# Attention kernel: VectorE's score cells from jobs further on, chains of eight, earlier casts and transposes

## The chip, the cores and the metric

The kernel runs on one core of a Trainium2 chip. The metric is device time in microseconds (us), from one execution of the whole program; lower is better. Eleven runs of the kernel before gave a median of 397.95 us (397.08 to 401.34).

A core has several engines that each run their own list of instructions in order and meet only through semaphores: TensorE (PE in the profile; PEld is its weight load), VectorE (DVE), ScalarE (ACT), GpSimd (POOL) and the DMA queues, of which SyncE's (SP) and POOL's are used here. An instruction that waits holds up all that stand behind it in its engine's list.

## The reference: grouped-query attention

```python
batch, n_q_heads, n_kv_heads, seq, head_dim = (8, 8, 2, 1024, 64)
for g in range(n_kv_heads):          # four q heads share one k and v head
    scores = scale * np.matmul(q_group, k_group.transpose(0, 1, 3, 2))
    scores_max = np.max(scores, axis=-1, keepdims=True)
    attn = np.exp(scores - scores_max)
    attn = attn / (np.sum(attn, axis=-1, keepdims=True) + 1e-08)
    output[:, q_start:q_end, :, :] = np.matmul(attn, v_group)
```

All is float32, the inputs are normal numbers times 0.1. The kernel leaves the maximum out, since the scores are small, and works in bf16 behind the loads.

## The kernel before, in words

**Jobs and cells.** A q head has 1024 rows; the even and the odd rows ("side") make two jobs of 512 rows, so 8 x 8 x 2 = 128 jobs. A job has eight cells, one for each 128 keys: 1024 cells. A cell's scores are one matmul (`score`, L351): 128 keys on the partitions, 512 q rows on the free axis, in one PSUM bank. The exponentials of a cell then serve as weights of four small matmuls against V with a column of ones (`output_mms`, L414, 128x65), which add up a job's output and its row sums in an `ops` bank. `normalise` (L427, L429) divides, and SP stores the job's 128 KB.

**Two engines make exponentials.** ScalarE takes pairs of cells (kind A; `exps`, L362, 128x1024 from the two-bank tile `aps`, of which there are two). VectorE takes single cells (kind D; `dps`, two banks): `exp_bits` (L371) turns a score into the bits of a power of two in a group tile `pd`, and when a group of GROUP = 4 cells is full, `exp_curve` corrects the mantissa of the whole group in four instructions, a chain: AND into `z` (L386), a line into `y` (L392), a product (L402) and a sum into `pd` (L406). Only then may the cells of the group go to PE.

**The planner.** `make_plan` decides on the host, ahead of the build, which cell goes to which engine and in which order each engine does its work. It keeps a time for PE, ACT and DVE, moves them on by fixed costs (`QK`, `PV`, `EXP`, `P1`, `NORM`, `CHAIN`), and picks the earliest step each time. Its times order the instructions; on the chip nothing waits for a time. In the kernel before, the cells are dealt out in order of their number: the next cell goes to ACT's tile or to DVE's bank, whichever is free first. LIVE_A, LIVE_D and PENDING bound the tiles in flight, and the last 14 cells (ONLY_A) go to ACT. Its 1024 cells become 412 pairs on ACT and 200 cells in 50 chains of four on DVE.

**Loads.** The first k, q and v heads come straight as float32, are cast on chip and turned by PE through the `dps` banks (`first_loads`). All other heads go the long way: a casting DMA from POOL's queue into a bf16 scratch in DRAM (`cast`, L248), from there two transposing DMAs on SP's queue for each head (`transpose`, L260), and for k a further four copies on POOL's queue into the zero-padded set `kset` (`place_k`, L268), for v two copies on SP's queue (`place_v`, L282). Two sets of k and v serve even and odd batches. Each load is put into the order some us of plan time ahead of the head's first cell. A cast that is put in after the first score also waits, through a dependency added by hand, for the last score issued ahead of it in the order ("pace"). In `first_loads` POOL also clears the second k set with two memsets (L309), ahead of all casts but the first.

Of the kernel before, what the change touches and what calls it, by code (L numbers as in the profile page):

```python
# [14 lines left out]
GROUP = 4  # L15


def make_plan(nj, nkc):
# [6 lines left out]
    QK, PV, EXP, P1, NORM = 0.214, 0.143, 0.925, 0.605, 0.57  # L25
    CHAIN = (0.73, 0.73, 1.26, 1.26)
    FROM_PE, FROM_ACT, FROM_DVE = 0.28, 0.18, 0.12
    LIVE_A, LIVE_D, PENDING, ONLY_A = 26, 6, 8, 14
    INF = 1e9
    n = nj * nkc  # L30
# [3 lines left out]
    nxt = 0  # L34
# [7 lines left out]

    def first_free(slots):
        return min(range(len(slots)), key=lambda s: slots[s])

    while normed < nj:
        best = None
        if nxt < n:
            ta = td = INF
            if open_a is not None:  # L50
                ta = max(pe, open_a["t"])
            elif live["A"] < LIVE_A:
                ta = max(pe, min(a_free))
            if pending < PENDING and nxt < n - ONLY_A and (cur or live["D"] < LIVE_D):
                td = max(pe, min(bank))
            t, to_d = (ta, 0) if ta <= td else (td, 1)
            if t < INF:
                best = min(best or (INF,), (t, 1 + to_d, "qk", to_d))
        for i, s in enumerate(open_jobs):
            for c in rem[s]:  # L60
                at = max(pe, ready.get(s * nkc + c, INF))
                if at < INF:
                    best = min(best or (INF,), (at, 3 + i, "pv", (s, c)))
        if len(open_jobs) < 2 and next_job < nj:
            at = max(pe, min(obank_free), min(ready.get(next_job * nkc + c, INF) for c in range(nkc)))
            if at < INF:
                best = min(best or (INF,), (at, 3 + len(open_jobs), "open", next_job))
        for q, p, kind in ((normq, 0, "norm"), (p1q, 1, "p1"), (chainq, 2, "chain")):
            if q:
                best = min(best or (INF,), (max(dve, q[0][0]), p, kind, 0))  # L70
        if cur and nxt >= n - ONLY_A and not p1q:
            best = min(best or (INF,), (dve, 9, "flush", 0))
        t, _, kind, arg = best
        if kind == "qk":
            cell = nxt
            nxt += 1
            pe = t + QK
            if not arg:
# [10 lines left out]
                if len(o["cells"]) == 2 or nxt >= n:  # L89
                    act = max(act, pe + FROM_PE)  # L90
                    ops.append((act, "exp", a_id, tuple(o["cells"])))
                    act += EXP * len(o["cells"]) / 2
# [5 lines left out]
            else:  # L98
                k = first_free(bank)
# [48 lines left out]
        else:  # L148
            _, g, cells, step = chainq.pop(0)
            ops.append((t, "chain", g, len(cells), step))  # L150
            dve = t + CHAIN[step] * len(cells) / GROUP
            if step + 1 < len(CHAIN):
                chainq.insert(0, (dve, g, cells, step + 1))
# [9 lines left out]
def kernel(  # L163
# [27 lines left out]
    PIECE = 256  # L191
    scale = 1.0 / math.sqrt(D)
# [15 lines left out]
    qT_pool = ctx.enter_context(tc.tile_pool(name="qTpool", bufs=8))  # L208
    kT_pool = ctx.enter_context(tc.tile_pool(name="kTpool", bufs=4))
    pa_pool = ctx.enter_context(tc.tile_pool(name="papool", bufs=26))  # L210
    pd_pool = ctx.enter_context(tc.tile_pool(name="pdpool", bufs=6))
# [76 lines left out]

    def first_loads():
# [216 lines left out]
```

The softmax here doesn't subtract the row's maximum and nothing guards it: scores larger than these inputs give would overflow.

## Time and profile before

| | |
|---|---|
| median of 11 runs | 397.95 us |
| the profiled execution's own time | 397.5 us |
| its span, first to last instruction | 395.6 us |
| busy: PE, DVE, ACT, POOL | 365.4, 375.9, 381.3, 87.4 us |
| exponentials on ACT | 412 instructions, 378.8 us |
| first exponential starts, last one ends | 8.18 us, 388.27 us |

The page gives for each engine its busy time, for each group of instructions the count, busy time and mean duration, and the idle time in front of them with what ended it. A group's mean can overlap with the next instruction's start, so a busy sum is smaller than count times mean. The timeline gives start and length of merged pieces in order of time. "SPq" and "POOL ... DMA_DIRECT2D" are the times in which a queue issues a transfer; its landing is later.

### The profile page before, as it was taken

Reading aid. Unit: us, or ns where it says so; the run is one execution under the profiler, and the core shown is the slowest. Engines: PE = TensorE matmul, PEld = TensorE weight load, DVE = VectorE, ACT = ScalarE, POOL = GpSimd, SP = SyncE. Lnnn points to the kernel's source line nnn. Section 1 sums busy time; section 2 is a strip of 40 time slices with the busy share of each in tenths; the row PEclk is TensorE's granted clock in tenths of the full one; section 3 lists DMA queues with packets and bytes.
Section 4 is the critical chain, followed back from the end, with each engine's and each line's share of the span. In section 5 each row is a group of like instructions: output and inputs, shape, how many; then the busy total and the mean of one; then the engine's idle time right before and its main releaser. Section 6 shows DMA issues by size and latency. Waiting matters only on the chain.

```text
span 395.6 us, 12683 instructions
## 1 busy us (share of the span) xinstructions
PE 365.4 (92%) x5043; PEld 232.9 (59%) x5132; DVE 375.9 (95%) x664; ACT 381.3 (96%) x415; POOL 87.4 (22%) x165
## 2 busy tenths in 40 slices
PE   4899999999999999999999999999999999999986
PEld 2455565565656556665656565565655666565655
DVE  4999999999999999999999999999999999999995
ACT  4999999999999999999999999999999999999992
POOL 5340404131041313113141040313113131210000
PEclk9999999999999999999999999999999999999999
DMA  4666967848577795758767677775955977573314
GB/s 106 108 122 110 152 100 136 140 94 150 103 136 133 114 152 99 129 108 151 118 114 127 105 124 146 137 124 109 149 95 117 155 131 138 95 127 82 68 28 94
DMA packets 134890, 46.72 MB, mean 118 GB/s; under 512 B 130848, under 2 KB 132384, under 8 KB 133344
## 3 DMA queue, kind: packets, MB, share of 16 engines
q1 hardware_dynamic: 129408, 29.52, 37.9%
q0 software_dynamic: 4896, 16.13, 28.3%
q8 instruction: 40, 0.66, 0.8%
q10 hardware_dynamic: 528, 0.26, 0.2%
q14 instruction: 18, 0.15, 0.1%
HBM read 27.13 MB, written 28.97 MB: 142 GB/s over the span
## 4 chain that ended last, share of the span: by engine, by line
ACT 67%; DVE 11%; PE 10%; issue 6%; DMA 3%; POOL 1%; SPq 0%
ACT pa L362 67%; PE ops L414 5%; PE aps L351 5%; DVE pd L371 3%; DVE y L402 2%; DVE pd L406 2%; DVE ost L429 1%; PE dps L351 1%; DVE y L392 1%; DMA vf<-in_v_dram 1%; DMA qT<-scr_q 1%; POOL kset L309 1%; DVE z L386 1%; DVE rec L427 1%; DMA scr_q<-in_q_dram 1%
## 5 line engine op out<-in xcount | busy, mean ns | idle before, releaser
L362 ACT ACTIVATE pa<-aps 128x1024 bf16<-128x1024 f32 x412 | 378.8, 1063 | 2.4 <-PE aps L351 1.7
L351 PE MATMUL aps<-qT,kset 128*128 128x512 bf16 x735 | 225.9, 379 | 16.0 <-ACT pa L362 13.6
L414 PEld LDWEIGHTS <-pa 128*128 128x128 bf16 x3296 | 134.6, 97 | 57.4 <-DVE ost L429 0.8
L414 PE MATMUL ops<-vset,pa 128*128 128x65 bf16 x3296 | 143.9, 194 | 3.4
L371 DVE TENSOR_SCALAR pd<-dps 128x512 uint16<-128x512 f32 x200 | 129.7, 681 | 1.9 <-PE dps L351 1.9
L351 PEld LDWEIGHTS <-kset 128*128 128x128 bf16 x1024 | 85.2, 97 | 66.7 <-issue 30.7
L248 POOL DMA_DIRECT2D scr_q<-in_q_dram x63 | 34.5, 547 | 173.7 <-PE aps L351 151.2
L351 PE MATMUL dps<-qT,kset 128*128 128x512 bf16 x200 | 64.3, 379 | 0.9
L406 DVE TENSOR_TENSOR pd<-pd,y 128x2048 uint16<-128x2048 uint16 x50 | 61.2, 1225 | 1.7
L402 DVE TENSOR_TENSOR y<-z,y 128x2048 f16<-128x2048 uint16 x50 | 61.2, 1225 | 1.7
L429 DVE TENSOR_TENSOR ost<-ops,rec 128x256 f32<-128x256 f32 x128 | 54.3, 424 | 4.4
L414 PEld LDWEIGHTS <-pd 128*128 128x128 bf16 x800 | 38.5, 97 | 29.8 <-DVE pd L406 8.1
L268 POOL DMA_DIRECT2D kset<-kT x60 | 32.4, 549 | 75.3 <-DMA kT<-scr_k 72.4
L414 PE MATMUL ops<-vset,pd 128*128 128x65 bf16 x800 | 45.3, 194 | 1.2
L392 DVE TENSOR_SCALAR y<-z 128x2048 f16<-128x2048 uint16 x50 | 34.3, 686 | 0.6
L386 DVE TENSOR_SCALAR z<-pd 128x2048 uint16<-128x2048 uint16 x50 | 34.2, 685 | 0.0
L427 DVE RECIPROCAL rec<-ops 128x4 f32<-128x4 f32 x128 | 22.4, 175 | 2.8 <-PE ops L414 2.3
L248 POOL DMA_DIRECT2D scr_v<-in_v_dram x15 | 7.7, 510 | 8.2 <-PE aps L351 7.4
L248 POOL DMA_DIRECT2D scr_k<-in_k_dram x15 | 8.3, 551 | 5.2 <-PE aps L351 4.0
L321 PE MATMUL dps<-ident,hk 128*128 128x128 bf16 x8 | 1.0, 311 | 5.0 <-DVE hk L313 5.0
L321 PEld LDWEIGHTS <-hk 128*128 128x128 bf16 x8 | 0.8, 140 | 5.0 <-DVE hk L313 5.0
L309 POOL MEMSET kset<- 64x2048 bf16 x2 | 3.6, 1798 | 0.1
(20 smaller groups left out, 9.7 us busy)
## 6 DMA issues: line engine op xcount, KB each, us to landing
out_dram<-ost SPq DMA_DIRECT2D x128, 128.0 KB, 3.0
scr_q<-in_q_dram POOLq DMA_DIRECT2D x63, 128.0 KB, 3.4
kset<-kT POOLq DMA_DIRECT2D x60, 64.0 KB, 2.6
qT<-scr_q SPq DMA_TRANSPOSE x126, 3.7
scr_k<-in_k_dram POOLq DMA_DIRECT2D x15, 128.0 KB, 4.2
scr_v<-in_v_dram POOLq DMA_DIRECT2D x15, 128.0 KB, 4.3
vset<-scr_v SPq DMA_DIRECT2D x30, 64.0 KB, 3.9
kT<-scr_k SPq DMA_TRANSPOSE x30, 3.3
```

The lines of the kernel that those rows point to most:

```text
L248: dma = nc.gpsimd.dma_start(out=scr.rearrange("(p f) -> p f", f=1024), in_=src.rearrange("(p s) d -> p (s d)", s=1024 // D),)
L268: nc.gpsimd.dma_start(out=ksets[b % 2][side * D : (side + 1) * D, g, side, parity * HALF : (parity + 1) * HALF], in_=kT[(b, g)][parity * D ...
L351: last_score[0] = nc.tensor.matmul(dst, lhsT=ksets[b % 2][:, h // HPG, side, c * 128 : (c + 1) * 128], rhs=qT[(b, h)], start=True, stop=Tr ...
L362: nc.scalar.activation(out=pt[:, 0:m], in_=psum.pop(("A", n))[:, 0:m], func=AF.Exp, scale=scale)
L371: nc.vector.tensor_scalar(out=groups[g][:, slot], in0=psum.pop(cell), scalar1=bits_scale, scalar2=bits_bias, op0=ALU.mult, op1=ALU.add,)
L386: nc.vector.tensor_scalar(out=z, in0=pd, scalar1=0x7F, scalar2=None, op0=ALU.bitwise_and)
L392: nc.vector.tensor_scalar(out=y, in0=temps[g][0], scalar1=CURVE_A / 128.0, scalar2=CURVE_B, op0=ALU.mult, op1=ALU.add,)
L402: nc.vector.tensor_tensor(out=y, in0=z, in1=y, op=ALU.mult)
L406: nc.vector.tensor_tensor(out=pd, in0=pd, in1=y, op=ALU.add)
L414: nc.tensor.matmul(ops_of[s][:, qs, :], lhsT=p_of[cell][:, qs * 128 : (qs + 1) * 128], rhs=vsets[b % 2][:, h // HPG, c, :], start=opens an ...
L427: nc.vector.reciprocal(out=rec, in_=o[:, :, D])
L429: nc.vector.tensor_tensor(out=ost, in0=o[:, :, 0:D], in1=rec.unsqueeze(2).to_broadcast([128, NQS, D]), op=ALU.mult,)
```

## The change

- `GROUP` is 8: a chain works on eight cells (4096 elements on each partition). `pd` tiles are 5 of twice the size in place of 6, `z` and `y` grow with them; `pa` has 28 buffers in place of 26, `qT` 10 in place of 8.
- The planner holds each job's cells to be done. ACT takes the next cell of the first job that has any left; VectorE takes the first cells left of a job that lies up to LEAD = 6 jobs further on (growing by one for each three jobs at the start), two of a job at most. A model of the first loads (`loaded`) keeps cells from being planned before 3.5 us, plus 3.0 us for each further q head. The planner's costs are new. Its order now has 411 pairs on ACT, and 202 cells on DVE in 25 chains of eight and a last chain of two.
- A head's first use is that of either job and either engine. Casts of q come 34 to 40 us of plan time ahead of it (28 before), transposes 17 to 21 (17), casts of k and v 46 and 42 ahead of the first use in their group (38 and 33), k's transposes 31 (first batch 19; 27 before), `place_k` 15 (first batch 8; 20 before).
- In `first_loads` k and q come in halves, PE first does 28 matmuls of the identity, which nobody reads (WARM), and the order of casts and copies is another. The memsets of the second k set leave `first_loads` and stand at 20 and 23 us of plan time.

```diff
-GROUP = 4
+GROUP = 8
@@ make_plan
+    LIVE_A, LIVE_D, PENDING, PER_JOB, LEAD, RAMP, AHEAD, FIRST_PV = 28, 5, 16, 2, 6, 3, 0.08, 2.0
+    FIRST_LOAD, EACH_LOAD = 3.5, 3.0
+    def loaded(j):
+        return FIRST_LOAD + EACH_LOAD * (j // 2 - 1) if j > 1 else 0.0
...
+        while job_a < nj and not todo[job_a]:
+            job_a += 1
+        lead = min(LEAD, job_a // RAMP)
+        job_d = max(job_d, job_a + lead)
+        while job_d < nj and (taken[job_d] >= PER_JOB or not todo[job_d]):
+            job_d += 1
...
+            cell = j * nkc + todo[j].pop(0)
@@ first_loads
-        for side in range(2):
-            nc.gpsimd.memset(ksets[1][(1 - side) * D : (2 - side) * D, :, side, :], 0.0)
+        warm = obanks[1].tile([128, 128], FP32, name="ops1")
+        for n in range(WARM):
+            nc.tensor.matmul(warm, lhsT=ident, rhs=ident, start=True, stop=True)
...
+        for half in halves:
+            nc.vector.tensor_copy(out=hk[:, half, 0:2, :], in_=fk[:, half])
+            turn_k(0, half)
+            nc.scalar.copy(
+                out=hq[:, half], in_=fq[:, half].rearrange("p c two d -> p c (two d)")
+            )
+            for c in range(NHC)[half]:
+                nc.tensor.transpose(tq[:, c * 128 : (c + 1) * 128], hq[:, c, :], ident)
@@ the order of the loads
+    for side in range(2):
+        at(20.0 + 3.0 * side, blank_k, side)
...
-            th = first_use[(b * H + h) * 2]
+            th = first_use[b * H + h]
             if (b, h) != (0, 1):
-                at(th - 28.0, cast, ("q", b, h), q[b, h])
+                at(th - (34.0 if b else 40.0), cast, ("q", b, h), q[b, h])
             for n in range(HALF // PIECE):
-                at(th - 17.0 + n, transpose_q, b, h, n)
+                at(th - (21.0 if b else 17.0) + n, transpose_q, b, h, n)
             if h % HPG == 0:
                 g = h // HPG
-                at(th - 38.0, cast, ("k", b, g), k[b, g])
-                at(th - 33.0, cast, ("v", b, g), v[b, g])
+                th = min(first_use[b * H + h + i] for i in range(HPG))
+                at(th - 46.0, cast, ("k", b, g), k[b, g])
+                at(th - 42.0, cast, ("v", b, g), v[b, g])
                 for n in range(HALF // PIECE):
-                    at(th - 27.0 + n, transpose_k, b, g, n)
+                    at(th - (31.0 if b else 19.0) + n, transpose_k, b, g, n)
                 for side in range(2):
                     for parity in range(2):
-                        at(th - 20.0, place_k, b, g, side, parity)
+                        at(th - (15.0 if b else 8.0), place_k, b, g, side, parity)
```

## The prediction

> **What bounds the kernel now.** I read the busy sums first, then the groups, then the timeline at both ends.
>
> ```profile
> PE 365.4 (92%) x5043; PEld 232.9 (59%) x5132; DVE 375.9 (95%) x664; ACT 381.3 (96%) x415; POOL 87.4 (22%) x165
> ...
> L362 ACT ACTIVATE pa<-aps 128x1024 bf16<-128x1024 f32 x412 | 378.8, 1063 | 2.4 <-PE aps L351 1.7
> L371 DVE TENSOR_SCALAR pd<-dps 128x512 uint16<-128x512 f32 x200 | 129.7, 681 | 1.9 <-PE dps L351 1.9
> L406 DVE TENSOR_TENSOR pd<-pd,y 128x2048 uint16<-128x2048 uint16 x50 | 61.2, 1225 | 1.7
> L402 DVE TENSOR_TENSOR y<-z,y 128x2048 f16<-128x2048 uint16 x50 | 61.2, 1225 | 1.7
> L392 DVE TENSOR_SCALAR y<-z 128x2048 f16<-128x2048 uint16 x50 | 34.3, 686 | 0.6
> L386 DVE TENSOR_SCALAR z<-pd 128x2048 uint16<-128x2048 uint16 x50 | 34.2, 685 | 0.0
> ```
>
> ACT and DVE look equally full, but ACT is the bound: its exponentials wait 2.4 us in all, 1.10 of it ahead of the first. One costs 378.8/412 = 0.919 us. The timeline gives the ends and the one real hole:
>
> ```profile
> 4.51 0.43 DVE L313 CAST hk<-f 128x512 bf16<-128x512 f32 x1 [1.42 <-DMA f<-in_k_dram]
> 4.86 0.29 DVE L314 CAST hk<-f 128x256 bf16<-128x256 f32 x1
> 5.82 0.63 PE L327 MATMUL dps<-ident,hq 128*128 128x128 bf16 x4
> 6.49 0.58 ACT L331 COPY qT<-dps 128x512 bf16<-128x512 bf16 x1 [0.94 <-PE dps L327]
> 6.57 3.65 POOL L309 MEMSET kset<- 64x2048 bf16 x2
> 7.13 1.67 PE L351 MATMUL aps<-qT,kset 128*128 128x512 bf16 x4 [0.67 <-ACT qT L331]
> 8.18 10.26 ACT L362 ACTIVATE pa<-aps 128x1024 bf16<-128x1024 f32 x11 [1.10 <-PE aps L351]
> 9.25 0.59 PE L351 MATMUL aps<-qT,kset 128*128 128x512 bf16 x2
> 13.05 2.39 SPq L260 DMA_TRANSPOSE qT<-scr_q  x2
> 18.43 0.59 PE L351 MATMUL aps<-qT,kset 128*128 128x512 bf16 x2 [0.74 <-DMA qT<-scr_q]
> 19.05 3.77 ACT L362 ACTIVATE pa<-aps 128x1024 bf16<-128x1024 f32 x4 [0.61 <-PE aps L351]
> ...
> 385.35 2.92 ACT L362 ACTIVATE pa<-aps 128x1024 bf16<-128x1024 f32 x3
> 389.24 2.63 PE L414 MATMUL ops<-vset,pa 128*128 128x65 bf16 x80
> 392.12 0.42 DVE L429 TENSOR_TENSOR ost<-ops,rec 128x256 f32<-128x256 f32 x1
> ```
>
> So the span is 8.18 (start) + 380.09 (ACT from 8.18 to 385.35 + 2.92 = 388.27) + 7.33 (tail) = 395.6. Of the middle, 378.8 is work, 0.61 the hole at 18.4, where PE waits for the third q head, and 0.7 small change. The run's own time is 397.5, 1.9 above its span; the median of the runs, 397.95, is 0.45 above that.
>
> **The middle: chains of eight.** The chain's cost for eight cells isn't in the trace. The two casts above (512 elements 0.427, 256 elements 0.286) give 0.145 us fixed for an instruction. So a 4096-element AND or line is 2 x 0.685 - 0.145 = 1.225, a product or sum 2 x 1.225 - 0.145 = 2.305. Bounds: no fixed part (1.37 and 2.45, no gain), or two fixed parts (1.08 and 2.16). Instructions fall from 200 to 104: 96 x 0.145 = 13.9 us less; two more cells cost 2 x (0.60 + 0.27 + 0.54) = 2.8 more (0.60 is the pitch of `exp_bits`: two take 1.28 where one takes 0.68). DVE's 375.9 becomes about 365 (between 361 and 379). None of it is on the path by itself: ACT's share only falls from 412 to 411 pairs, 0.92 us. DVE's gain turns into idle time, and its slack against ACT's 378 grows from about 2 to about 13 us. Only at the high end of the bounds would DVE tie with ACT.
>
> The rule on VectorE's fixed latency of an instruction ("VectorE: DVE Perf Modes", section on the TRN2 errata) has a measured fixed term of about 150 cycles, 0.156 us by an estimate at its 0.96 GHz, a little more than my 0.145; the DVE sum would be 1 us lower, and the time the same.
>
> PE keeps its 1024 scores and 4096 output matmuls. At 0.21 a score (two take 0.59 where one takes 0.38) and 0.031 an output matmul (80 in 2.63, of which 0.19 is one's length) that is 215 + 127 = 342 of ACT's 378. D cells now lie up to seven jobs ahead of ACT's, so their outputs are ready when PE comes to them; the 8.1 us that output weights wait for `pd` should go, hidden already.
>
> **The start.** q's second half of cast, transposes and copy sets the first score. The loads are the same bytes; a half of the q cast is about 0.35 (0.62 less 0.27), so it ends near 5.3 where the whole ended at 5.56. But 28 matmuls of the identity now stand ahead on PE: they can begin when the identity is done (2.34) and take about 0.10 each (eight transposes in 0.77 of weight loads), to 5.1 or 5.4. Eight transposes behind them end at 6.2 to 6.5, against 6.45 before, so the copy gains 0 to 0.25, and I take 0.1. Then the scores: the first four take 1.67, (1.67 - 0.38)/3 = 0.43 apart, a later pair is 0.21 apart, and the granted clock of the profile reads full in both stretches. PE had then worked since 5.0. If the early work makes the first pair run at the later pitch, the first exponential comes 0.2 to 0.4 sooner. I take 7.7 in all (7.3 to 8.4, the last if the halves land 0.2 later and nothing is gained).
>
> For the clock, "TensorE: Matmul & The Clock Gate" (Part 1) says that PE runs at half rate until about 3.4 us of sustained work, in a window that runs free; work from 2.4 would end the slow state near 5.8, ahead of the first score. By the rule the first exponential is near 7.6; by the rows alone, with no lift, near 8.0.
>
> **The first loads.** This is the largest unknown. Without the memsets POOL is free at 6.5 (or 7.0, since v is issued one half-load later on SP) where it was at 10.17, so the third q head's cast and transposes move 3.2 to 3.65 us up: landed by 18.29 before, by 14.6 to 15.1 after. Its first D score stands behind the ninth pair of A scores: issued from 7.7 + 7 x 0.919 + 0.43 = 14.6; ACT starves only when it is later than about 7.7 + 9 x 0.919 - 0.6 - 0.43 = 14.9. So 0 to 0.2 is lost. SP then transposes without a break at 1.2 us each: the fourth head lands near 17.4 to 18.0 (needed 17.3, starving from 18.1). The second k group lands on 19 to 20.5, its copies (2.3 to 4.2 us to landing in the trace) at 22.8 to 24.7; needed at 22.8, starving from 23.6: 0 to 1.1. The sixth q head: issued at 24.3, landed 27.8 to 28.5, starving from 28.2: 0 to 0.3. Against it, nine casts now run back to back from 6.8 where six ran from 10.2; those six already stretched a transpose from 2.35 us to 4.7. I take 0.8 lost in place of the 0.61 (0 to 4). What is queued behind a late transfer is all of PE's list, A scores too.
>
> Later casts are issued 34 us ahead and transposes 21, so a late POOL (72.4 us of waits for `kT` before, now landed in time) costs nothing. The memsets, 3.65 us on POOL, stand in front of casts with such leads: hidden.
>
> A rule speaks against the longer chain: "SBUF — State Buffer" (the "DVE blocks DMA" trap) says that POOL can't write descriptors while DVE runs a two-port operation. By it a cast could come up to one AND later. In the trace a POOL issue for q takes 0.547 us in the mean, and a whole AND of 1.2 us is small beside the lead of 34, so the time is the same with it and without.
>
> **The tail.** Before, after ACT's end PE still had 24 cells of outputs to do; 7.33 us to the span's end, of which 392.54 to 395.6 = 3.06 is the last store. In the new order PE has only the last pair's outputs left: 8 x 0.031 + 0.19 = 0.44, reciprocal and product 0.64, small hand-overs 0.15, store 3.06: 4.3 (bounds 4.1 and, if PE is late as before, 7.3).
>
> **Sum.** 7.7 + 411 x 0.919 (377.9) + 0.7 + 0.8 + 4.3 = 391.4, against 395.6: 4.2 less. On the profiled run's 397.5 that is 393.3, on the median's scale 393.8.
>
> **The rivals.**
> 1. The loads come in time and the warm start is full: 7.3 + 377.9 + 0.7 + 4.1 = 390.0, 392.4 on the median's scale. The 14.9 against 14.6 speaks for it, the transposes' stretch under casts against.
> 2. The start starves: three of the heads or k copies each land a us or more late, 4 us in all: 397. Nine casts in a row speak for it; the planned 3.0 us for a head, against 2.4 of SP issue, against.
> 3. Slower: VectorE's long instructions hold PE. A product holds both `dps` banks 2.3 us where it was 1.2; a D score issued on PE then blocks the A scores behind it. ACT has one pair in hand, 0.92 less the 0.6 that a pair takes to come, so 0.3 spare. There are 50 such instructions: the gain of 4.2 is gone at 0.08 each; if each costs 0.2 beyond the spare, 10 us, the time is 404. For it: two banks only. Against it: the planner puts a D score where it holds its bank to be free, and its costs for DVE (2.32, 1.264) are no lower than mine, so PE should seldom come early; and with 1.225 the same pattern left ACT 0.7 us of gaps in 380.
> 4. The order brings nothing: ACT's pairs are the bound, and one less is 0.92 us; with tail and start as before, 397.0, no change.
>
> **Numbers.** Chances: forecast 0.55, rival 1 0.18, rival 2 0.10, rival 3 0.10, rival 4 0.07. A measurement tells about 0.3% (1.2 us) from no change, so faster is below 396.75: forecast, rival 1 and a part of the others, 0.79; within 0.3% 0.09; slower 0.12. The range of 391.5 to 398 leaves out most of rival 3 and the far end of rival 1; the forecast's own range is 392 to 396.
>
> **What would show it.** Right: 411 exponentials, first at about 7.7, last ending near 387, no wait of over 1 us in front of them; AND 1.2 and product 2.3 us; DVE busy near 365; 4.3 us from the last exponential to the end. Wrong: ACT waiting for `aps` behind PE's wait for DVE (rival 3), or for `qT` and `kset` before 30 us (rival 2); a tail of 7 us.

## The result and the profile after

The kernel after the change takes **402.76 us** in the median (12 runs, 400.31 to 405.4) against 397.8 for the kernel before, measured beside it and pooled over 47 runs. The ratio is 1.0126, with an interval of 1.0109 to 1.0142: slower by about 5 us, where 4.2 us less were forecast. The profiled execution took 402.9 us with a span of 400.8. Here and below a ratio leaves out executions over 1.5% above the fastest of their kernel, while medians and ranges hold all of them.

The busy sums and the groups of the page, after the change (count, busy us, mean ns, idle time in front):

```profile
PE 365.0 (91%) x5070; PEld 233.6 (58%) x5160; DVE 367.5 (92%) x571; ACT 381.6 (95%) x415; POOL 90.8 (23%) x165
...
L407 ACT ACTIVATE pa<-aps 128x1024 bf16<-128x1024 f32 x411 | 378.9, 1059 | 10.7 <-PE aps L396 9.8
L416 DVE TENSOR_SCALAR pd<-dps 128x512 uint16<-128x512 f32 x202 | 131.4, 682 | 10.2 <-PE dps L396 9.5
```

VectorE's sum fell from 375.9 to 367.5 us, ScalarE has 411 pairs with the same busy time as before, and nothing in the busy column tells why the kernel is slower. The idle column does: ScalarE's exponentials wait 10.7 us where they waited 2.4, and VectorE's `exp_bits` waits 10.2 for a D score. Both wait for PE. The timeline of ACT in the kernel after (start, length, pieces merged; in brackets the idle time ahead of a piece and what ended it) shows where:

```profile
7.76 8.64 ACT L407 ACTIVATE pa<-aps 128x1024 bf16<-128x1024 f32 x9 [0.68 <-PE aps L396]
24.34 1.02 ACT L407 ACTIVATE pa<-aps 128x1024 bf16<-128x1024 f32 x1 [7.94 <-PE aps L396]
25.62 1.02 ACT L407 ACTIVATE pa<-aps 128x1024 bf16<-128x1024 f32 x1 [0.26 <-PE aps L396]
26.91 14.82 ACT L407 ACTIVATE pa<-aps 128x1024 bf16<-128x1024 f32 x16 [0.26 <-PE aps L396]
42.38 13.01 ACT L407 ACTIVATE pa<-aps 128x1024 bf16<-128x1024 f32 x14 [0.65 <-PE aps L396]
55.59 341.07 ACT L407 ACTIVATE pa<-aps 128x1024 bf16<-128x1024 f32 x370 [0.21 <-ACT pa L407]
```

One hole of 7.94 us stands at 16.4, 1.4 us of smaller ones follow, and from 55.59 on 370 exponentials run without a gap at 341.07/370 = 0.922 us. So the span is 7.76 (start) + 388.9 (ACT, to 396.66) + 4.14 (tail), and 9.3 of the middle is idle. The time was lost in the first 56 us; the rest of the kernel comes within 1 us of what the forecast said.

The chain of waits of the kernel after, cut to 5 to 30 us (start, length, what):

```profile
6.98 3.24 DMA scr_q<-in_q_dram
...
10.23 1.29 SPq L286
...
11.56 10.81 DMA qT<-scr_q
22.38 0.04 issue
22.42 1.03 PE dps L396 x2
23.45 0.85 PE aps L396 x2
```

The third q head's cast landed in 3.24 us, promptly. Its second transpose, issued at 11.56, landed at 22.38, 10.81 us later; in the kernel before the same transfer took 4.09 (14.20 to 18.29), by its chain of waits from 8 to 20 us:

```profile
10.17 2.86 DMA scr_q<-in_q_dram
...
13.05 1.10 SPq L260
...
14.20 4.09 DMA qT<-scr_q
```

The score that waits for it is a D score, and all A scores stand behind it in PE's list. The POOL timeline of the kernel after, in the same stretch:

```profile
6.98 0.52 POOL L274 DMA_DIRECT2D scr_q<-in_q_dram  x1
...
8.93 1.44 POOL L274 DMA_DIRECT2D scr_q<-in_q_dram  x3
...
12.83 0.49 POOL L274 DMA_DIRECT2D scr_q<-in_q_dram  x1 [1.03 <-PE aps L396]
13.51 0.49 POOL L274 DMA_DIRECT2D scr_q<-in_q_dram  x1 [0.19 <-PE aps L396]
14.68 1.12 POOL L274 DMA_DIRECT2D scr_k<-in_k_dram  x1 [0.68 <-PE aps L396]
```

and its DMA view from 6 to 24 us (queues with packets, MB and share of the 16 engines; issues with count, KB each and median us to landing):

```profile
q0 software_dynamic: 416, 1.70, 69.3%
q1 hardware_dynamic: 2880, 0.66, 21.6%
...
scr_q<-in_q_dram POOLq DMA_DIRECT2D x8, 128.0 KB, 5.0
...
qT<-scr_q SPq DMA_TRANSPOSE x8, 7.4
```

Thirteen casts went into POOL's queue between 6.98 and 15.8 us, where the kernel before had six from 10.17 to 13.6. While they last, SP's transposes take 7.4 us in the median, and the late one 10.8. The changed profile thus names a suspect, a row of casts that keeps the transposes from landing. It does not prove it, since the change also moved which score comes first. The experiments take the two apart.

The waiting costs a little beyond its own length. PE's timeline of the kernel after, behind the hole:

```profile
22.42 1.03 PE L396 MATMUL dps<-qT,kset 128*128 128x512 bf16 x2 [7.42 <-DMA qT<-scr_q]
23.25 1.06 PE L396 MATMUL aps<-qT,kset 128*128 128x512 bf16 x2
```

Two scores take 1.03 where two took 0.59 in the kernel before, so PE came back at half its pitch, and the two holes of 0.26 are ScalarE waiting for it. The granted clock (third number from the end in a line of busy times by stretch, 1.00 in the stretches from 0 to 20 us) shows it as well:

```profile
20.00:24.30 4.30, 1.88 (x5) 0.72 (x6) 1.24 (x2) 0.00 (x0) 0.00 (x0) 0.56 0.69 103
```

The trace's clock record has half clock from 20.55 to 27.38 us and full clock on either side.

### The profile page after: what moved, and what is told of

Same layout as the page of the kernel before. It is cut to its first block, busy times and chain, and to the rows that moved or that the text cites. A ratio compares the mean times of both kernels' runs of the same rounds, so it can differ in the third digit from the quotient of the medians.

```text
span 400.8 us, 12618 instructions
## 1 busy us (share of the span) xinstructions
PE 365.0 (91%) x5070; PEld 233.6 (58%) x5160; DVE 367.5 (92%) x571; ACT 381.6 (95%) x415; POOL 90.8 (23%) x165
## 4 chain that ended last, share of the span: by engine, by line
ACT 57%; PE 21%; DVE 9%; issue 7%; DMA 5%; SPq 1%; POOL 0%
ACT pa L407 57%; PE aps L396 10%; PE ops L459 8%; PE dps L396 4%; DVE pd L416 3%; DMA qT<-scr_q 3%; DVE pd L451 2%; DVE z L431 1%; DVE ost L474 1%; DMA vf<-in_v_dram 1%; DVE rec L472 1%; DMA scr_q<-in_q_dram 1%; DVE y L437 1%; SPq L286 0%; DVE y L447 0%
## 5 line engine op out<-in xcount | busy, mean ns | idle before, releaser
L407 ACT ACTIVATE pa<-aps 128x1024 bf16<-128x1024 f32 x411 | 378.9, 1059 | 10.7 <-PE aps L396 9.8
L459 PE MATMUL ops<-vset,pa 128*128 128x65 bf16 x3288 | 148.6, 194 | 2.8
L416 DVE TENSOR_SCALAR pd<-dps 128x512 uint16<-128x512 f32 x202 | 131.4, 682 | 10.2 <-PE dps L396 9.5
L396 PE MATMUL dps<-qT,kset 128*128 128x512 bf16 x202 | 72.4, 385 | 9.9 <-DMA qT<-scr_q 7.4
L274 POOL DMA_DIRECT2D scr_q<-in_q_dram x63 | 31.3, 497 | 139.4 <-PE aps L396 109.5
L447 DVE TENSOR_TENSOR y<-z,y 128x4096 f16<-128x4096 uint16 (+1 forms) x26 | 57.7, 2220 | 0.1
L451 DVE TENSOR_TENSOR pd<-pd,y 128x4096 uint16<-128x4096 uint16 (+1 forms) x26 | 57.7, 2220 | 0.1
L294 POOL DMA_DIRECT2D kset<-kT x60 | 36.6, 620 | 59.5 <-DMA kT<-scr_k 58.8
L459 PE MATMUL ops<-vset,pd 128*128 128x65 bf16 x808 | 42.1, 194 | 0.4
L431 DVE TENSOR_SCALAR z<-pd 128x4096 uint16<-128x4096 uint16 (+1 forms) x26 | 32.4, 1247 | 0.0
L437 DVE TENSOR_SCALAR y<-z 128x4096 f16<-128x4096 uint16 (+1 forms) x26 | 30.9, 1187 | 0.0
L340 PE MATMUL ops<-ident 128*128 128x128 bf16 x28 | 3.2, 311 | 2.4 <-POOL ident masks.py:199 2.4
```

The costliest lines, as they stand in the source:

```text
L274: dma = nc.gpsimd.dma_start(out=scr.rearrange("(p f) -> p f", f=1024), in_=src.rearrange("(p s) d -> p (s d)", s=1024 // D),)
L294: nc.gpsimd.dma_start(out=ksets[b % 2][side * D : (side + 1) * D, g, side, parity * HALF : (parity + 1) * HALF], in_=kT[(b, g)][parity * D ...
L396: last_score[0] = nc.tensor.matmul(dst, lhsT=ksets[b % 2][:, h // HPG, side, c * 128 : (c + 1) * 128], rhs=qT[(b, h)], start=True, stop=Tr ...
L407: nc.scalar.activation(out=pt[:, 0:m], in_=psum.pop(("A", n))[:, 0:m], func=AF.Exp, scale=scale)
L416: nc.vector.tensor_scalar(out=groups[g][:, slot], in0=psum.pop(cell), scalar1=bits_scale, scalar2=bits_bias, op0=ALU.mult, op1=ALU.add,)
L431: nc.vector.tensor_scalar(out=z, in0=pd, scalar1=0x7F, scalar2=None, op0=ALU.bitwise_and)
```

## The experiments

Two reasons stand against each other. **Row:** the casts that are issued early and together hold the transposes back, for as long as the row lasts. **Demand:** VectorE's lead asks for the third head sooner (a D score behind nine pairs of A scores, where before an A score came behind eleven), and with it any landing would be late. A third stands beside them, rival 3 of the prediction: long chains hold PE. Each ratio is against the kernel before, run on the same chip. "Hole" is ScalarE's idle stretch ahead of the first pair behind the third q head's landing, in the profiled execution. The row is counted from the third head's cast up to the last cast that POOL issued before that head landed. Holes and landings are those of one execution for each kernel; where runs scatter, that execution is not always near the median.

**1. The change, with the casts of the first batches issued later.** The order of the cells stays as it is. Seven casts are issued without a break and three more, with gaps, before the head lands: a row of ten.

```diff
-at(th - (34.0 if b else 40.0), cast, ("q", b, h), q[b, h])
+at(th - (28.0 if b else 20.0), cast, ("q", b, h), q[b, h])
-at(th - 46.0, cast, ("k", b, g), k[b, g])
-at(th - 42.0, cast, ("v", b, g), v[b, g])
+at(th - (36.0 if b else 26.0), cast, ("k", b, g), k[b, g])
+at(th - (30.0 if b else 22.0), cast, ("v", b, g), v[b, g])
```

> The changed kernel with the casts of the first batches later again: 6 casts stand ahead of the first score where 10 do. Theory (casts in a row keep the transposes from moving): the third q head lands by 15 us where it was 22.4, the hole in the exponentials at 16.4 us falls from 7.9 to under 1 us, and the time to 402.8 - 8 = 394 to 395. Rival (VectorE's cells from jobs further on ask for heads sooner than SP's queue can turn them, whatever the casts do): a hole of 4 us or more stays in one place or in several, and the time is above 398.

Measured: 399.65 us (396.8 to 402.8, 10 runs; 397.8 in the profiled one), ratio 1.0043 (1.0009 to 1.0077), 3.1 us less than the change. ACT's timeline:

```profile
19.31 1.02 ACT L407 ACTIVATE pa<-aps 128x1024 bf16<-128x1024 f32 x1 [2.76 <-PE aps L396]
```

The hole went from 7.94 to 2.76, the third head landed at 17.70 instead of 22.38. The direction is the row's, but the landing was expected by 15 us and the time under 395; ten casts are still a row. A time above 398 was also named for the rival, so this run alone does not part the two.

**2. The change, with the casts of the first batch as early as in the change and only the others later.** Nine casts are issued without a break and two more before the head lands: a row of eleven (`28.0 if b else 40.0`, `36.0 if b else 46.0`, `30.0 if b else 42.0` in the same three lines).

> The changed kernel with the casts of batch 1 alone later, those of batch 0 as in the change: 9 casts in a row where 12 or 13 ran. Theory (the row of casts): a hole between those of the changed kernel (7.9) and of the paced one, near 3 to 4 us: 397 to 399. Rival (the demand): as the changed kernel, 402 to 403, or as the paced one if that is also above 398.

Measured: 402.52 us (398.8 to 403.9), ratio 1.0102 (1.0047 to 1.0156). By the median this is no different from the change, where 397 to 399 was expected; the profiled execution, the fastest of four (398.8), has a hole of 5.25 and a landing at 19.63.

**3. The kernel before, with its casts issued earlier and nothing else.** Nine casts are in the row.

```diff
-at(th - 28.0, cast, ("q", b, h), q[b, h])
+at(th - 40.0, cast, ("q", b, h), q[b, h])
-at(th - 38.0, cast, ("k", b, g), k[b, g])
-at(th - 33.0, cast, ("v", b, g), v[b, g])
+at(th - 46.0, cast, ("k", b, g), k[b, g])
+at(th - 42.0, cast, ("v", b, g), v[b, g])
```

> The kernel before, with its casts alone put earlier by as much as in the change (q 40, k 46, v 42 us ahead): 9 casts run in a row where 6 did. VectorE's cells stay with their jobs. Theory (the row of casts): three more casts at about 0.7 us each, so the third head lands near 20.5 us in place of 18.3 and the hole grows from 0.6 to about 2.5 us: 399.5 to 400.5. Rival (the demand from jobs further on): nothing changes, 397.5 to 398.3.

Measured: 401.25 us (399.1 to 401.5), ratio 1.0073 (1.0047 to 1.0099). In the profiled execution, the fastest of four, the third head landed at 19.99 instead of 18.29, 1.70 later, and the exponentials behind it start at 20.75 instead of 19.05, 1.70 later too. The holes grew from 0.61 to 2.0: 1.12 for the third head, and 0.62 and 0.27 ahead of it, where PE was still at its slow pitch (full clock begins at 11.47 us in this trace, at 8.48 in that of the kernel before). Issuing loads sooner makes this kernel slower all by itself.

**4. The kernel before, with six more casts that nobody reads.** Six heads of the last batch go to a scratch of their own, behind the first four casts of the row (two of q, one of k, one of v), which makes a row of twelve. The cells, their order and all other loads are as before.

```diff
+def idle_casts():
+    for n in range(6):
+        scr = scr_pool.tile([S * D], BF16, name="scr_x")
+        nc.gpsimd.dma_start(
+            out=scr.rearrange("(p f) -> p f", f=1024),
+            in_=q[7, n].rearrange("(p s) d -> p (s d)", s=1024 // D),
+        )
+at(-5.5, idle_casts)
```

> The kernel before with six more casts of other q heads into scratch that nobody reads, issued between the first v cast and the fifth q head's. Nothing else is changed. Theory (each cast in the row holds the transposes back by what three more casts did in the early-cast run, (2.0 - 0.6)/3 = 0.47 us, to the 0.65 us between landings): the third head lands at 21 to 22 us, the hole grows by 2.8 to 3.9 us, time 400.5 to 402. If transposes and casts share the DMA engines evenly, the third head lands within 1 us of 18.3 and the time is 397.5 to 399.

Measured: 405.31 us (405.02 to 406.07), ratio 1.0197 (1.018 to 1.0214): 7.7 us more for six idle casts, twice what was expected. ACT's timeline from 8 to 32 us, of this kernel:

```profile
8.13 10.35 ACT L362 ACTIVATE pa<-aps 128x1024 bf16<-128x1024 f32 x11 [1.10 <-PE aps L351]
24.64 1.02 ACT L362 ACTIVATE pa<-aps 128x1024 bf16<-128x1024 f32 x1 [6.15 <-PE aps L351]
26.37 1.02 ACT L362 ACTIVATE pa<-aps 128x1024 bf16<-128x1024 f32 x1 [0.71 <-PE ops L414]
28.08 1.02 ACT L362 ACTIVATE pa<-aps 128x1024 bf16<-128x1024 f32 x1 [0.68 <-PE aps L351]
29.54 2.86 ACT L362 ACTIVATE pa<-aps 128x1024 bf16<-128x1024 f32 x3 [0.44 <-PE aps L351]
```

its DMA view from 10 to 24.6 us:

```profile
scr_x<-in_q_dram POOLq DMA_DIRECT2D x6, 128.0 KB, 6.3
...
qT<-scr_q SPq DMA_TRANSPOSE x4, 7.0
```

and its chain of waits:

```profile
10.25 2.89 DMA scr_q<-in_q_dram
...
13.16 1.10 SPq L260
...
14.31 9.14 DMA qT<-scr_q
```

This shows the row as a cause without the change's planner: the third head's cast lands as before (2.89 us; 2.86 before), its transpose takes 9.14 where it took 4.09, and the holes come to 8.0 us against 0.61. The landing is 5.16 us later (23.45 for 18.29), 0.9 us for each cast that was put in. With the three holes behind the first, in which PE is at its slow pitch again (half clock from 22.27 to 29.10 us), the holes grow by 7.4/6 = 1.2 us for each.

"DMA: Bandwidth & Descriptors" of the Trainium skill (section "Issuing engines are not separate DMA queues") says that transfers of all issuing engines run on the same 16 DMA engines and interleave with each other. The first half agrees with this run: work that POOL issued slowed work that SP issued. An even interleaving is not seen: from 16 to 20 us the packets of POOL's queue took 99.4% and those of SP's queue 15.3%, and only from 22 to 24 us, when POOL's had come down to 40.8%, did SP's rise to 110.5% (shares of the 16 engines' time; the times of packets overlap, so sums over 100% occur). How the DMA engines choose between the two queues no run here shows.

**5. The change, with the row kept and VectorE's demand slowed.** The lead grows by one for each six jobs, and D cells come from the current job and its lead alone until the sixth job. Eleven casts stay in the row.

```diff
-LEAD, RAMP = 6, 3
+LEAD, RAMP = 6, 6
-if job_d < nj and job_d <= job_a + lead + 1 and pending < PENDING:
+if job_d < nj and job_d <= job_a + lead + (job_a > 5) and pending < PENDING:
```

> The changed kernel with only the planner's lead growing more slowly (one job for each six, and no job beyond the lead until the sixth): the first score of the third head comes behind 12 pairs in place of 9, that of the second k group 1.8 us later. Some 11 casts still run in a row. Theory (the row of casts sets when the transposes land, and the demand only sets how much of it is felt): the third head still lands near 21 us, the hole is 3 to 5 us in place of 7.9, and the time 398 to 400. If the demand alone were the cause, the hole would be gone and the time 394 to 396; if neither mattered, it would stay at 402 to 404.

Measured: 405.08 us (403.1 to 406.3), ratio 1.0177 (1.0148 to 1.0206). The first hole went down to 3.53, within what was expected for it, with the third head landed at 20.64; twelve pairs came before it where the change has nine. So demand is the second factor. Number 2 also has a row of eleven; its head landed 1.0 us sooner (19.63) and its hole was still 1.7 longer, since ScalarE ran dry at 16.35 there, after nine pairs, and at 19.07 here, after twelve. The time missed the expectation, and is longer than the change's, because new holes of 0.5 to 2.4 us appeared from 130 to 353 us, again with PE waiting for `qT`. They return in numbers 9 to 12.

**6. Shorter chains.** Number 1 with `GROUP = 4` and ten `pd` tiles (`LIVE_D = 10`): the change's order of cells with the chains of before.

> The paced kernel with chains of four (ten tiles of half the size): 414 pairs on ACT, 196 cells in 49 chains. If the longer chain gives time only through the pairs that it moves, this is 3 x 0.92 = 2.8 us slower than the paced one: 396 to 398. If VectorE at four is full and holds PE (as its 0.145 us for each of some 90 more instructions would make it, 13 us), it is 5 us or more slower: over 399. If long products hold PE, it is faster than the paced one.

Measured: 402.57 us (402.5 to 406.7), ratio 1.0152 (1.0099 to 1.0205), against 399.65 for number 1. VectorE's busy time is 373.4 (366.5 in number 1), the planner gives ScalarE 414 pairs, three more, and the tail is 6.4 us where it was 4.1; the hole at the start is 3.89 (2.76). So the chains of eight were a gain, through the cells that the planner could give to VectorE and through the tail, and nothing here speaks for rival 3.

**7. The change, with the loads of the first two batches spread out.** Three casts are issued without a break and four more, with gaps, before the head lands: a row of seven (q 13.5, 26 and 34 us ahead in the first, second and further batches, k 18, 28 and 46, v 10, 24 and 42; transposes later to match). One run as it is, one without the 28 matmuls of the identity (`WARM = 0`), one with the planner's costs set to the chain's measured ones (`P1` 0.60; fixed parts of AND, line and product 0.13, 0.15 and 0.14 in place of 0.20, 0.20 and 0.16).

> The changed kernel with the first two batches' casts and transposes spread out: three casts stand ahead of the first score (10 in the change), each later one is held by a score and comes some 3.5 us ahead of its transposes. Planner, chains, warm-up and tail are those of the change. Theory (casts in a row keep the transposes from moving): the third head lands by 14.5 us, no hole over 1 us is left, the span is 7.7 + 379 + 1 + 4.1 = 391.8 and the time 393 to 395. Rival (jobs further on ask sooner than SP's queue turns, about 2.5 us a head): one or more holes of 2 us or more between 15 and 30 us, 396 or more.

> The same without the 28 matmuls of the identity. If they bring the first pair of scores to the later pitch, the first exponential is 0.2 to 0.4 us later here and the time the same within what can be told; if their place ahead of the transposes costs as much, there is no difference at all.

> The spread-out kernel with the planner's costs of VectorE's chain as the profile shows them (AND 0.13 + 0.133 a cell, line 0.15 + 0.133, products 0.14 + 0.267, exp_bits 0.60): 409 pairs on ACT, 206 cells on VectorE. If ACT's pairs are the bound and VectorE has room (367 us busy in the change), it is 2 x 0.92 = 1.8 us faster than the spread-out kernel: 391.5 to 393. If VectorE's long instructions hold PE once VectorE is full, it is no faster.

Measured: 404.82 us (1.0171, 1.0129 to 1.0213), 404.15 (1.0164, 1.0128 to 1.0199) and 401.69 (1.0098, 1.0071 to 1.0125). In the first of them the third head landed at 16.07, 6.3 us sooner than in the change, and the holes there are 0.88 and 1.09. But the loads that were not issued in the row come later in one of their own. ACT's timeline of this first kernel:

```profile
48.19 1.94 ACT L407 ACTIVATE pa<-aps 128x1024 bf16<-128x1024 f32 x2 [6.76 <-PE aps L396]
```

and POOL's, from 26 to 46 us:

```profile
26.79 0.49 POOL L274 DMA_DIRECT2D scr_q<-in_q_dram  x1 [0.60 <-PE aps L396]
...
39.93 0.50 POOL L274 DMA_DIRECT2D scr_q<-in_q_dram  x1
40.41 0.49 POOL L274 DMA_DIRECT2D scr_k<-in_k_dram  x1
```

and SP's:

```profile
38.43 1.12 SPq L286 DMA_TRANSPOSE qT<-scr_q  x1
...
40.26 3.70 SPq L286 DMA_TRANSPOSE qT<-scr_q  x3
```

The eighth head's cast is the one at 26.79: in the order of the loads it stands ahead of `place_k`, and was in time. Its two transposes, put only 10 us of plan time ahead of the first use and behind other transposes, copies and stores on SP's list, were issued at 38.43 and 41.44. There they met the next row, four casts issued from 39.93 to 41.86, and the second took 4.72 us to land. The hole moved from 16 to 41 us and cost 6.76. A few casts less at the start are no gain when the heads behind are turned late, into the next row.

The run without the warm-up answers another question: its first exponential is at 7.30, 0.29 sooner than with it (7.59), but its third at 9.86 and not at 9.43, because its scores run at the slow pitch (four take 1.86, against 1.02). Between these two executions the warm-up is worth about 0.4 us, though not at the first exponential.

**8. Number 7, with a slower model of the first loads** (`FIRST_LOAD, EACH_LOAD = 4.2, 4.3`, and the first batch's last q head cast 18 us ahead in place of 13.5), with the change's costs and with the measured ones.

> The spread-out kernel with two edits: the cast of the first batch's last q head stands 5 us of plan time earlier (in the spread-out kernel it stood behind the copies of the next batch's k, which wait for a transpose, and the head came at 45 us), and the planner's model of the first loads is 4.2 us plus 4.3 for each further head in place of 3.5 and 3.0, so that VectorE's first cells of the third and fourth head come 1.0 and 2.7 us later. Theory (late heads are the whole loss; the pairs, chains and tail give what was forecast): holes of 2 us at most in all, span 7.7 + 378.6 + 2 + 4.1 = 392.4, time 393 to 396. Rival (the loss is bound to VectorE's lead, however the loads are spread): 5 us of holes or more, 398 and up.

> The same with the measured costs of VectorE's chain in the planner: 409 pairs, 206 cells on VectorE. If ACT is the bound, 1.8 us faster than the run beside it: 391 to 394.5. If VectorE, fuller, holds PE, the same or slower.

Measured: 403.24 us (1.0133, 1.011 to 1.0157) and 402.7 (1.012, 1.0081 to 1.016). The first hole is 1.76 and 1.39, the second 5.14 and 5.34: the eighth head's second transpose was issued at 39.83, met five casts issued from 40.9 to 43.3 and landed at 45.41. Casting that head sooner did not remove the hole, which agrees with its cast having been in time in number 7.

**9. The loads at the distances of the kernel before, and a slow lead.** Six casts are in the row again; the lead grows by one for each twelve jobs. The transposes and `place_k` of the first two batches stand as they did before, too. Two runs: the change's costs, and the measured ones.

```diff
-LEAD, RAMP = 6, 3
+LEAD, RAMP = 6, 12
-if job_d < nj and job_d <= job_a + lead + 1 and pending < PENDING:
+if job_d < nj and job_d <= job_a + lead + (lead > 0) and pending < PENDING:
-at(th - (34.0 if b else 40.0), cast, ("q", b, h), q[b, h])
+at(th - (38.0 if b > 1 else 28.0), cast, ("q", b, h), q[b, h])
...
-at(th - 46.0, cast, ("k", b, g), k[b, g])
-at(th - 42.0, cast, ("v", b, g), v[b, g])
+at(th - (48.0 if b > 1 else 38.0), cast, ("k", b, g), k[b, g])
+at(th - (44.0 if b > 1 else 33.0), cast, ("v", b, g), v[b, g])
```

> The changed kernel with the lead growing by one job for each twelve (none before the twelfth job) and the loads of the first two batches at the distances of the kernel before (28, 17, 38, 33, 27, 20, 15), later ones further ahead (38, 24, 48, 44, 33, 17). Six casts run ahead of the first score, as before, and the third head is needed 2.8 us later than in the change. Theory (a row of casts against an early demand): holes of 0 to 1.5 us in all, span 7.7 + 378.6 + 1 + 4.1 = 391.4, time 393 to 395. Rival (chains of eight or VectorE's lead lose time by themselves): no hole at the start, but ACT loses 3 us or more later on, 397 and up.

> The same with the measured costs of VectorE's chain in the planner: 410 pairs, 204 cells on VectorE. If ACT is the bound, 0.9 us faster than the run beside it; if VectorE, fuller, holds PE, no faster.

Measured: 405.3 us (1.0179, 1.0149 to 1.021) and 401.95 (1.0093, 1.0061 to 1.0125). The start is clean, in ACT's timeline of the first of the two:

```profile
7.44 2.89 ACT L407 ACTIVATE pa<-aps 128x1024 bf16<-128x1024 f32 x3 [0.68 <-PE aps L396]
10.50 8.36 ACT L407 ACTIVATE pa<-aps 128x1024 bf16<-128x1024 f32 x9 [0.17 <-PE dps L396]
19.01 31.55 ACT L407 ACTIVATE pa<-aps 128x1024 bf16<-128x1024 f32 x34 [0.15 <-PE aps L396]
```

But 9.9 us of holes come between 178 and 282 us, in the stretch where the lead is still growing. Its waits from 150 to 290 us (us, times, longest):

```profile
PE dps L396 <- DMA qT<-scr_q: 9.3, 6, 4.0
...
SPq L286 <- PE aps L396: 18.1, 15, 2.0
```

PE waits for q heads, and SP, which is to transpose them, waits for PE to be done with one of the ten `qT` tiles. That suggests tiles.

**10. Number 9 with more room.** `qT` 16 tiles (10), scratch 8 (6), casts and transposes from the third batch on issued a little sooner (q 42 and 28, k 54 and 40); again with both sets of costs.

> The slow-lead kernel with more room for the later heads: 16 qT tiles in place of 10, 8 scratch tiles in place of 6, and from the third batch on q cast 42 and turned 28 us ahead, k cast 54 and turned 40 ahead. The slow-lead run lost nothing at the start and 9.5 us between 178 and 282 us, in waits of scores for qT, while SP's transposes waited for scores, that is for a free qT tile. Theory (late loads are the only loss of the whole change): the holes in the middle fall under 1 us, span 7.6 + 378.6 + 1 + 4.1 = 391.3, time 393 to 394.5, and the change's other parts give what was forecast. Rival (something in VectorE's cells or chains loses time there): the holes stay, 398 and up.

> The same with the measured costs of VectorE's chain in the planner, 410 pairs and 204 cells: 0.9 us faster than the run beside it if ACT is the bound, 392 to 393.5.

Measured: 399.83 us (394.1 to 401.8, 12 runs; 0.9981, 0.9947 to 1.0014) and 397.6 (393.1 to 402.4, 12 runs; 0.9967, 0.9938 to 0.9995): level with the kernel before by these ratios; the first's median over all executions is 0.5% above it, the second's equal. In the profile of the first, 401.75 us, a new wait shows: stores stand behind transposes on SP, and the output tiles run out (`ost` waited 8.3 us for six stores).

**11. Number 10 with 24 output and reciprocal tiles** (10 each).

> The run with more room, with 24 output tiles and 24 reciprocals in place of 10. There VectorE's normalising waited 8.3 us, in six pieces, for the store of an earlier output: SP's stores stood behind its transposes. Theory (every loss left is a wait on SP's or POOL's queue, none is one of the chains or cells): these waits go, holes under 1.5 us in all, time 393 to 395. Rival: holes of 4 us or more stay, 397 and up.

> The same with the measured costs of VectorE's chain in the planner, 410 pairs: up to 0.9 us faster than the run beside it, 392 to 394.5.

Measured: 400.44 us (1.0059, 1.0037 to 1.0082) and 401.59 (1.009, 1.0075 to 1.0105; one execution of the second is told of at the end). The holes between 200 and 275 us are back (1.31, 1.73 and 2.61), with PE waiting for `qT` once more. More tiles alone don't remove them. These are readings of the first kernel.

**12. A lead that stays at two until near the end.** Number 9's loads, number 11's tiles, and:

```diff
-lead = min(LEAD, job_a // RAMP)
+lead = min(LEAD, min(2, job_a // RAMP) + max(0, job_a - 90) // 5)
```

> The slow-lead kernel with the lead held at two jobs from the 24th to the 90th job and growing to six only near the end, and with 16 qT, 8 scratch and 24 output tiles. Pairs (411) and cells as in the change. Theory (holes in the middle come from SP's queue being crowded while the lead grows, since each step of it asks for a head early): holes of 1.5 us at most in all, span 7.6 + 378.6 + 1.5 + 4.3 = 392, time 393 to 395, a faster kernel than the one before. Rival (the chains or cells themselves, or the loads at any lead): holes of 4 us or more, 397 and up.

Measured: **394.86 us** (394.2 to 395.4, five runs), ratio 0.993 (0.9916 to 0.9943): faster than both kernels. Its chains are the change's chains of eight, its pairs the same 411. The page:

```profile
PE 364.0 (93%) x5070; PEld 232.5 (59%) x5160; DVE 366.8 (93%) x571; ACT 381.4 (97%) x415; POOL 92.6 (24%) x165
...
L407 ACT ACTIVATE pa<-aps 128x1024 bf16<-128x1024 f32 x411 | 378.7, 1060 | 1.7 <-PE aps L396 0.8
```

and ACT's timeline over the whole span:

```profile
7.77 80.40 ACT L407 ACTIVATE pa<-aps 128x1024 bf16<-128x1024 f32 x87 [0.68 <-PE aps L396]
88.33 299.16 ACT L407 ACTIVATE pa<-aps 128x1024 bf16<-128x1024 f32 x324 [0.17 <-PE aps L396]
```

ScalarE runs from 7.77 to 387.49 with 0.17 us of one hole, and the tail is 4.9. Its span of 392.4 is 1 us from the 391.4 that the forecast's terms gave for the change. So most of the forecast gain, 3.0 of 4.2 us, is there once no head comes late; not all of the change, since this lead is smaller.

**The rows side by side.** Casts in the row, start of the first cast, landing of the third q head, the time between the two, and the hole that waits for the head, in us of the profiled execution:

| kernel | casts | first cast | landed | between | hole |
|---|---|---|---|---|---|
| order of cells before: before | 6 | 10.17 | 18.29 | 8.12 | 0.61 |
| before, casts earlier (3) | 9 | 10.23 | 19.99 | 9.76 | 1.12 |
| before, six idle casts (4) | 12 | 10.25 | 23.45 | 13.20 | 6.15 |
| order of cells after: loads spread (7) | 7 | 7.26 | 16.07 | 8.81 | 0.88 |
| casts later (1) | 10 | 7.26 | 17.70 | 10.44 | 2.76 |
| half of them later (2) | 11 | 7.33 | 19.63 | 12.30 | 5.25 |
| the change | 13 | 6.98 | 22.38 | 15.40 | 7.94 |
| the change, slower demand (5) | 11 | 7.34 | 20.64 | 13.30 | 3.53 |

The time from the first cast to the landing follows the length of the row in both orders of cells, by about 1 us for each cast, although the third head's cast is at the row's front in all of them.

Nearly the same landing costs 1.12 in number 3 (19.99) and 5.25 in number 2 (19.63). That is the demand. ScalarE ran dry at 19.63 in number 3 and at 16.35 in number 2, where two pairs fewer come first (1.84 us) and it had started 0.8 sooner. And behind the landing its next pair came after 0.76 us in number 3 and after 1.98 in number 2, where two D scores stand ahead of the A scores.

## Why the prediction was wrong

**Chains of eight: right.** The AND took 1.280 us and the line 1.218 where 1.225 was taken, the product 2.282 for 2.305; VectorE's sum is 367.5 for about 365. As forecast the pairs fell by one and the gain became slack; number 6 shows that it is worth three pairs and some of the tail against chains of four in the same order. The pair that fell away saved nothing: 411 exponentials took 378.9 us where 412 took 378.8. POOL's waits for `kT`, held to be gone, still come to 58.8 us; they are off ScalarE's path.

**The start: right, with some luck.** The first exponential came at 7.76 for 7.7, and the first four scores took 1.02 us where they took 1.67 before. The profile's rows read a clock of 1.00 here in both kernels, which says nothing: the trace's clock record begins, at full clock, only at 6.90 us in the kernel after and at 8.48 in the kernel before. That PE's early work brings this forward, number 7 shows by leaving it out (10.22 without, 5.96 with it). Over all profiles but that of the single execution told of at the end, the record begins at 5.20 to 8.27 us in the 15 with the early work and at 8.48 to 11.47 in the four without. In three of the 15 (number 1, the third kernel of number 7, the first of number 10) it came only after the first score: four scores took 1.41 to 1.59 us, and the first exponential came at 8.15 to 8.24.

**The tail: right.** 4.14 us for 4.3.

**Rival 3: refuted.** From 55.59 us on, 370 pairs ran 0.922 us apart with products of 2.28 us all along; no wait of PE for VectorE shows on ScalarE's path.

**The first loads: the failed step.** It closed with "I take 0.8 lost in place of the 0.61 (0 to 4)"; 9.3 us were lost in holes. All else together is 400.8 - 9.3 = 391.5, where the forecast without its 0.8 has 390.6; the 0.9 between them is the pair that saved nothing. Of the prediction's cases, rival 2 named the mechanism, heads landing late at the start, and priced it at 4 us; it got 0.10.

Three parts of that step were wrong. First, the landing of the third head was worked out by moving the old one up by the 3.2 to 3.65 us that POOL is free sooner, so 14.6 to 15.1. It came at 22.38: what sets it is not only when its own cast starts but how many casts follow. Second, the text did name the counterweight, "those six already stretched a transpose from 2.35 us to 4.7", and then treated that stretch as a size, not as a rate. Number 4 gives the rate, 0.9 us of later landing for each further cast. By that rate, an estimate, nine casts put the landing at 17.2 to 17.7 and thirteen at 20.6 to 21.1. The trace of before held a hint: its last cast, issued at 13.1, had landed by 17.8 (4.7 at most), and the second transpose, issued at 14.2, landed at 18.29, just behind it. Third, the count: nine casts were assumed and thirteen ran in the row. The hand-made dependency on a score held only the last three of them, for 1.03, 0.19 and 0.68 us.

A fourth point was right in its arithmetic and wrong in its weight. Nine pairs were to cover the third head, and ScalarE did run dry after nine, at 7.76 + 8.64 = 16.4. With such a deadline everything rests on one landing, and that landing, which no row of the trace showed, was costed near the lower of its bounds.

**What stays open.** Why the larger lead makes q heads late between 130 and 353 us (numbers 5, 9 and 11) is not settled. Waits of SP for free `qT` tiles are part of it in number 9, but more tiles alone did not remove the holes; a lead of two together with the tiles did, and a lead of two without them was not run. Nor is it shown why the kernel after scatters over 5 us (400.31 to 405.4), where 134 of 137 executions of the kernel before lie between 397.08 and 398.8; the kernel of number 12, whose loads come in time, has 394.2 to 395.4. The mean granted clock of an execution goes along with it in part: 0.998 to 1.0 in the 90 of the kernel before that list it, 0.999 to 1.0 in number 12, and 0.985 (the slowest) to 0.996 (the fastest) in the kernel after. In number 10's second kernel those at 0.999 and up took 393.06 to 396.93 us, those at 0.996 took 397.22 to 402.36. What makes one execution lose more than another stays open.

## What to carry to other kernels

Issuing a load sooner is not free for the loads ahead of it: a row of large casts on POOL's queue delays the small transposes of SP's queue for as long as the row lasts, so issue what is needed first, keep what is needed later out of its way, and look for where the postponed loads meet again. When a change moves loads, don't shift an old landing by the earlier start; count the transfers that are under way beside it and multiply by what one of them costs. When a planner takes work from further on, the deadline of every load moves with it, and a larger lead makes those deadlines harder.

## What the runs showed of the hardware that was not expected

- Six casts of 128 KB into memory that nobody reads made a kernel of 398 us 7.7 us slower (ratio 1.0197, 1.018 to 1.0214), by holding back two transposes from a queue of another engine: 9.14 us to landing in place of 4.09. The thirteen casts of the change made it 10.81.
- After 7.42 us without work PE came back at half its pitch (two scores 1.03 us, where they took 0.59) and ScalarE waited for it twice more. "TensorE: Matmul & The Clock Gate" of the Trainium skill (Part 1) says that idle time lowers PE's rate until it has worked for a while; this stretch agrees, and so does the granted clock, at half from 20.55 to 27.38 us.

One execution of the second kernel of number 11 took 938.24 us, where its others took 400.73 to 401.87. The group of A scores on its page:

```profile
L396 PE MATMUL aps<-qT,kset 128*128 128x512 bf16 x820 | 566.9, 818 | 0.1
```

A score takes 818 ns in the mean over the whole execution, where the median of one is 377 in the kernel after. The 1.0 that stands for its granted clock says nothing, since its trace has no clock record. It happened once in the runs of this case, and its cause is not known.
